# Hybrid decoder block on one Trainium2 core: the low part of every second MLP weight chunk made by an adding transfer instead of a subtraction

## Chip, cores and metric

The kernel runs on one core of one Trainium2 chip. The metric is device time in microseconds (us), the median of several executions; lower is better. Everything is float32 at the interface. The times of the kernel before are 1257.58, 1258.53 and 1259.71 us.

## The reference

One layer of a hybrid decoder trunk, for 256 tokens (and 16 learned meta tokens ahead of them) of width 2048:

```
u = RMSNorm(h)
[z_pool | v_conv | g_conv | gate_a | gate_b] = u @ W_in
A: causal multi-scale pooling, per-group map, scale, projection to 2048
B: GLU -> depthwise conv (31 taps) -> LayerNorm -> swish -> projection to 2048
m = sigmoid(gate_a) * A + sigmoid(gate_b) * B ;  h += RMSNorm(m @ W_o)
h += RMSNorm(W_down (relu(W_up RMSNorm(h)))^2)
```

The change touches only the last line, the MLP. `W_up` is 2048 x 8192 and `W_down` is 8192 x 2048, 64 MB each in float32.

## The kernel before

**Products in split precision.** Each float32 weight is split exactly into a high part (rounded to the short format `float32r`) and a low part (the rest), and so is each activation. A product is made of three: high by high, high by low, low by high. In `mm2` (L312 and L317) the high weights meet both parts of the activations in one matmul of 512 columns and the low weights meet the high activations in one of 256; in `block_t` (L651) there are three matmuls of 512 columns for every 128 rows of weights.

**Chunks.** All weights come in one fixed list, `stream`, of chunks of 1 MB: 128 partitions x 2048 floats. An MLP chunk holds 512 rows (4 tiles of 128) by 512 columns, so in HBM it is made of runs of 2 KB, and on chip each partition has one run of 8 KB. There are 217 chunks, numbered from 0; the MLP's are 89 to 216. The inner width of the MLP is taken in four pieces; each has 16 chunks of `W_up` (4 columns of 4 chunks, the "up" stages) and then 16 chunks of `W_down` (the "dn" stages).

**Life of a chunk.** `open_chunk` (L136) takes room in three pools of three buffers each, `raw`, `hi` and `lo`, which rotate by chunk number. SyncE's queue (SP) loads `raw` from HBM (L153). ScalarE (ACT) copies `raw` to `hi` with rounding (L156). VectorE (DVE) makes `lo = raw - hi` (L159). TensorE (PE) then reads `hi` and `lo`. `fetch` (L176) returns the next chunk for PE, and at the same time opens and splits the one two places further on. So the split of chunk c stands in the program ahead of PE's work on chunk c-2, and its `hi` and `lo` go into the room of chunk c-3: ACT waits for PE's end with chunk c-3, and PE then works through chunks c-2 and c-1 before it needs chunk c.

**Order.** Every engine issues in the order of the text (`manual_schedule`). SP issues only the chunk loads in this part of the kernel, one after the other: the load of chunk c+3 waits until the room of `raw` c is no longer read. ACT has, beside the casts to `hi`, in the up stages the copies of finished accumulators (`half_up`, L351) and the high parts of the MLP's activations (`f_act`, L358). GpSimd (POOL) is idle in the MLP; it issues a few transfers earlier in the kernel (L213, L679 to L683).

The last eight chunks (209 to 216) and the first eight of the MLP (89 to 96) are not touched by the change.

Of the kernel before, what the change touches and what calls it, by code (L numbers as in the profile page):

```python
# [11 lines left out]
ALU = mybir.AluOpType  # L12
# [3 lines left out]
CK = 4          # rows of 128 in one weight chunk  # L16
CW = 512        # columns of one weight chunk
# [5 lines left out]
def hybrid_block(ctx: ExitStack, tc: tile.TileContext, ins: dict, out: bass.AP):  # L23
# [6 lines left out]
    NT = T // P                     # token tiles  # L30
    KD = D // P                     # feature tiles of the model width
# [11 lines left out]
    KP = PW // P                    # feature tiles of the pooling branch  # L43
    KC = CC // P                    # feature tiles of the convolution branch
    FF = w_up.shape[1]
    PAD = TAPS - 1 - M              # zeros ahead of the first meta token
# [19 lines left out]
    # every engine issues in the order of this text  # L66
    ctx.enter_context(tc.manual_schedule())

# [1 line left out]
    pending = []  # L70
    late = []                       # what the Scalar engine does after the next chunk's split
    LATER = (0, None)               # what follows waits for the next call
    FETCH = (0, late)               # what follows waits for what is late
# [7 lines left out]
    def drain(us=None):  # L81
        """as much of it as fits in us, with what earlier calls left over"""
        credit["us"] += us or 0.0
        while pending and (us is None or credit["us"] >= pending[0][0]):
            cost, f = pending[0]
            if f is late and late:
                if us is not None:
                    break
                flush()
            pending.pop(0)  # L90
            if callable(f):
                f()
                if us is not None:
                    credit["us"] -= cost
            elif f is None and us is not None:
                break
        credit["us"] = min(credit["us"], pending[0][0]) if pending else 0.0

# [1 line left out]
    def columns(w, k0, nk, c0, shape=(CK, CW)):  # L100
        """chunks of rows k0.. (nk tiles), columns c0.., in their order"""
        ck, cw = shape
        return [(w[(k0 + kc) * P:(k0 + kc + ck) * P, c0:c0 + cw]
                 .rearrange("(k p) c -> p k c", p=P), shape) for kc in range(0, nk, ck)]
# [20 lines left out]
    # two chunks of w_up that are split early, into room that is free for a while  # L125
    spare = {len(stream) + 1: "s0", len(stream) + 2: "s1"}
    for i in range(NP):
        for h in range(NB):
            stream += columns(w_up, 0, KD, i * D + h * CW)
        for n in range(NB):  # L130
            stream += columns(w_down, i * KD, KD, n * CW)
    FIRST = KD // HALF[0]           # chunks of the first product, taken piece by piece
    opened = []                     # chunks under way
    at = {"n": 0}

    def open_chunk():  # L136
        n = at["n"]
        at["n"] += 1
        src, (rows, width) = stream[n]
        raw = raws.tile([P, CK * CW], F32, tag="raw", name=f"raw_{n}")  # L140
        if n in spare:
            both = big.tile([P, 2, CK * CW], F32R, tag=spare[n], name=f"parts_{n}")
            hi, lo = both[:, 0, :], both[:, 1, :]
        else:
            hi, lo = (parts.tile([P, CK * CW], F32R, tag=tag, name=f"{tag}_{n}")
                      for tag in ("hi", "lo"))
        raw, hi, lo = (t.rearrange("p (k c) -> p k c", k=rows) for t in (raw, hi, lo))
        pieces = rows if n < FIRST + 1 else 1
        k = rows // pieces
        loads = 4 if n < FIRST else 1  # L150
        for i in range(loads):
            sl = slice(i * rows // loads, (i + 1) * rows // loads)
            nc.sync.dma_start(raw[:, sl, :], src[:, sl, :])  # L153

        def high(sl):
            nc.scalar.copy(hi[:, sl, :], raw[:, sl, :])  # L156

        def low(sl):
            nc.vector.tensor_sub(lo[:, sl, :], raw[:, sl, :], f32(hi[:, sl, :]))  # L159

        def piece(i):
            def f():
                sl = slice(i * k, (i + 1) * k)
                high(sl)
                low(sl)
            return f
        todo = [piece(i) for i in range(pieces)]
        if n in spare:
            todo = [lambda: high(slice(0, rows)), lambda: low(slice(0, rows))]
        opened.append((hi, lo, todo))  # L170
# [5 lines left out]
    def fetch(ahead=2):  # L176
        """the next chunk, with the ones after it under way"""
        for c in range(ahead + 1):
            if c == len(opened) and at["n"] < len(stream):
                open_chunk()  # L180
            if c < len(opened):
                split_pieces(c)
        flush()
        return opened.pop(0)[:2]

# [7 lines left out]
    def warm_up(func):  # L193
        """loads the table of func"""
        nc.scalar.activation(warm, ones[:, 0:1], func)
# [21 lines left out]
    def rows_to_columns(rows, n, name):  # L217
        """vectors, P of their elements to a column"""
        pv = misc_tile(f"pv_{name}")
        nc.tensor.transpose(pv[:, :n], rows[:n, :], ident[:n, :n])  # L220
        nc.vector.tensor_copy(vecs[:, cols[name]:cols[name] + n], pv[:, :n])
# [20 lines left out]
    # the Tensor engine's clock rises with work: some of it until the data is there  # L242
# [25 lines left out]
    def rsqrt(r, q, var):  # L268
        """r: 1/sqrt(var), with q the table's root, after one of Newton's steps on it"""
# [32 lines left out]
    def mm3(acc, hi, lo, act, k, cs, first, last):  # L302
        """acc[:, :N] += w.T @ act, for the tokens in act or the last T of them, of the two
        parts of each"""
# [15 lines left out]
    def mm2(acc, hi, lo, act, k, cs, first, last):  # L320
        """acc[:, :T] + acc[:, T:] += w.T @ act, for the last T tokens, with the high part of
        the weights against both parts at once"""
# [9 lines left out]
    def project(act, nk, evac, name, mm=mm2, width=CW, shape=HALF, fill=0.0):  # L332
        """the next columns of act @ w; evac(j, acc) takes each P of them"""
# [14 lines left out]
    def halves(acc, name):  # L348
        """the two halves' sum, on chip"""
# [48 lines left out]
    # the first product: each tile of x as it comes, each chunk piece by piece  # L398
    def pieces_to(n):
        """the splits of the first n pieces"""  # L400
# [70 lines left out]
    def level(g):  # L471
        """trailing sums of 2 ** (g + 1) tokens, for the groups from g on"""
# [32 lines left out]
    ln = {}  # L505

    def sum_items(key, dst, src):
        """the sum over all channels, in every partition; dst is overwritten"""
# [19 lines left out]
    QW = 4                          # channel tiles to an instruction  # L528
# [134 lines left out]
    def project_t_but_two(act, nk, accs):  # L663
        """all but the last two chunks, which are returned"""
# [7 lines left out]
    def project_t_two(act, nk, accs, two, t):  # L672
        """the last two chunks, for one tile of tokens"""
# [12 lines left out]
    class Norm:  # L686
        """1/rms of the tokens of a tile, from the sums of squares of its blocks"""
# [10 lines left out]
        def steps(self, t, last=None):  # L698
            """1/rms, in steps: the root's table, and one of Newton's steps on it"""
# [51 lines left out]
    u2 = m                          # whose first tiles are read no more by then  # L751

    def u2_tiles(t0, n, k0, nk):
        """feature tiles k0.. of h1, for n tiles of tokens from t0 on: to features x tokens;
        returns what makes the parts of it"""
# [31 lines left out]
    # the first tokens are done two chunks earlier than the last ones in the last columns of w_o,  # L787
    # and go ahead of them in the first ones of w_up
# [46 lines left out]
    def up_high(kc, t):  # L835
        """the high parts of a chunk, for a tile of tokens"""
# [49 lines left out]
    # the norm's scale of a token goes through relu^2 as its square  # L886
# [37 lines left out]
    def finish_down(t, cuts):  # L924
        """the residual and the way out, in pieces of columns"""
# [13 lines left out]
    # the last columns: the first tokens are done three chunks earlier than the last ones, which  # L939
    # take their columns in two halves  # L940
# [65 lines left out]
```

## Time and profile before

| | |
|---|---|
| median of 3 runs | 1258.53 us |
| span of the profiled execution, first to last instruction | 1256.1 us |
| what lies around the span, against that median | 2.4 us |
| PE busy | 1242.3 us, 99% |
| DVE busy | 822.0 us, 65% |
| ACT busy | 544.7 us, 43% |
| chunk loads by SP (queue q1) | 230.70 MB, 57.7% of the 16 DMA engines' span |

The span is that of one execution under the profiler. No separate time of that execution is given outside the span, so the 2.4 us are the difference to the median of the unprofiled runs. A busy time counts an engine's instructions; its share says nothing about who waits for whom. That is read from the chain that ended last, from the timeline, and from the waits. The share of a DMA queue is the time that its packets took, divided by the time of all 16 engines: share times window is the time that the work would take with all 16 engines busy on it.

### The profile page before, as it was taken

Reading aid. Unit: us, or ns where it says so; the run is one execution under the profiler, and the core shown is the slowest. Engines: PE = TensorE matmul, PEld = TensorE weight load, DVE = VectorE, ACT = ScalarE, POOL = GpSimd, SP = SyncE. Lnnn points to the kernel's source line nnn. Section 1 sums busy time; section 2 is a strip of 40 time slices with the busy share of each in tenths; the row PEclk is TensorE's granted clock in tenths of the full one; section 3 lists DMA queues with packets and bytes.
Section 4 is the critical chain, followed back from the end, with each engine's and each line's share of the span. In section 5 each row is a group of like instructions: output and inputs, shape, how many; then the busy total and the mean of one; then the engine's idle time right before and its main releaser. Section 6 shows DMA issues by size and latency. Waiting matters only on the chain.

```text
span 1256.1 us, 18048 instructions
## 1 busy us (share of the span) xinstructions
PE 1242.3 (99%) x7682; PEld 1118.4 (89%) x7682; DVE 822.0 (65%) x1002; ACT 544.7 (43%) x595; POOL 6.1 (0%) x18
## 2 busy tenths in 40 slices
PE   8999999999999999999999999999999999999997
PEld 7999999999999988898888888888888888888886
DVE  5799986999887764585654456544475544556555
ACT  6633334443457444455433335433344433435432
POOL 1000000000000000000000000000000000000000
PEclk9999999999999999999999999999999999999999
DMA  8655556555656865646556656556656556666551
GB/s 244 208 184 179 168 175 195 175 195 177 193 168 212 290 203 194 207 137 199 179 191 200 194 177 198 175 194 200 189 180 200 177 194 200 178 191 198 180 192 68
DMA packets 155346, 237.39 MB, mean 189 GB/s; under 512 B 3986, under 2 KB 79058, under 8 KB 154737
## 3 DMA queue, kind: packets, MB, share of 16 engines
q1 hardware_dynamic: 153856, 230.70, 57.7%
q0 software_dynamic: 768, 4.35, 0.9%
q8 instruction: 60, 0.98, 0.3%
q10 hardware_dynamic: 640, 1.19, 0.3%
q14 instruction: 22, 0.17, 0.0%
HBM read 234.12 MB, written 2.10 MB: 188 GB/s over the span
## 4 chain that ended last, share of the span: by engine, by line
PE 98%; DMA 1%; DVE 0%; ACT 0%; DVEq 0%; ACTq 0%; issue 0%
PE acc_dn L651 26%; PE acc_up L312 19%; PE acc_gate L307 15%; PE acc_up L317 10%; PE acc_o L651 5%; PE acc_v L307 4%; PE acc_z L307 4%; PE acc_g L307 4%; PE acc_po L307 4%; PE acc_co L307 4%; PE acc_f_last L651 2%; PE acc_o_last L651 2%; PE xt L256 1%; DMA m_in<-in_meta_dram 1%; PE ht L759 0%; PE xt L254 0%
## 5 line engine op out<-in xcount | busy, mean ns | idle before, releaser
L159 DVE TENSOR_TENSOR lo<-raw,hi 128x2048 fp32r<-128x2048 f32 (+1 forms) x236 | 495.0, 2100 | 360.2 <-ACT hi L156 360.0
L156 ACT CAST hi<-raw 128x2048 fp32r<-128x2048 f32 (+1 forms) x236 | 413.9, 1757 | 583.6 <-PE acc_dn L651 191.1
L312 PE MATMUL acc_up<-m,hi 128*128 128x512 f32 (+1 forms) x1008 | 344.8, 395 | 0.0
L651 PE MATMUL acc_dn<-hi,f_act 128*128 128x512 f32 x960 | 295.9, 389 | 0.0
L317 PE MATMUL acc_up<-m,lo 128*128 128x256 f32 x992 | 265.8, 281 | 0.0
L312 PEld LDWEIGHTS acc_up<-m,hi 128*128 128x128 f32 x1008 | 183.3, 188 | 39.5
L651 PEld LDWEIGHTS acc_dn<-hi,f_act 128*128 128x128 f32 x960 | 180.2, 188 | 37.1
L317 PEld LDWEIGHTS acc_up<-m,lo 128*128 128x128 f32 x992 | 186.2, 189 | 6.3
L651 PE MATMUL acc_dn<-lo,f_act 128*128 128x512 f32 x480 | 186.7, 389 | 0.0
L307 PE MATMUL acc_gate<-u,hi 128*128 128x256 f32 x1024 | 182.9, 283 | 0.0
L307 PEld LDWEIGHTS acc_gate<-u,hi 128*128 128x128 f32 x1024 | 157.5, 189 | 0.1
L307 PE MATMUL acc_gate<-u,lo 128*128 128x256 f32 x512 | 144.7, 283 | 0.0
L375 DVE SCALAR_TENSOR_TENSOR c<-a,taps,c 128x256 f32<-128x256 f32 x240 | 115.2, 482 | 6.1
L651 PEld LDWEIGHTS acc_dn<-lo,f_act 128*128 128x128 f32 x480 | 90.1, 188 | 18.9
L307 PEld LDWEIGHTS acc_gate<-u,lo 128*128 128x128 f32 x512 | 97.0, 189 | 0.0
L651 PE MATMUL acc_o<-hi,m 128*128 128x512 f32 x192 | 59.3, 389 | 0.0
L307 PE MATMUL acc_v<-u,hi 128*128 128x272 f32 x256 | 50.8, 296 | 0.0
L307 PE MATMUL acc_g<-u,hi 128*128 128x272 f32 x256 | 48.4, 288 | 0.0
L307 PE MATMUL acc_z<-u,hi 128*128 128x272 f32 x256 | 48.3, 288 | 0.0
L307 PE MATMUL acc_po<-y,hi 128*128 128x256 f32 x256 | 45.5, 280 | 0.0
L307 PE MATMUL acc_co<-s_act,hi 128*128 128x256 f32 x256 | 45.3, 279 | 0.0
L651 PEld LDWEIGHTS acc_o<-hi,m 128*128 128x128 f32 x192 | 36.0, 188 | 7.5
(221 smaller groups left out, 1151.5 us busy)
## 6 DMA issues: line engine op xcount, KB each, us to landing
raw<-in_w_up_dram SPq DMA_DIRECT2D x64, 1024.0 KB, 5.4
raw<-in_w_down_dram SPq DMA_DIRECT2D x64, 1024.0 KB, 5.1
raw<-in_w_in_dram SPq DMA_DIRECT2D x54, 1024.0 KB, 5.1
raw<-in_w_o_dram SPq DMA_DIRECT2D x16, 1024.0 KB, 5.1
raw<-in_w_pool_out_dram SPq DMA_DIRECT2D x8, 1024.0 KB, 5.3
raw<-in_w_conv_out_dram SPq DMA_DIRECT2D x8, 1024.0 KB, 6.3
x_in<-in_x_dram SPq DMA_DIRECT2D x4, 512.0 KB, 8.8
raw<-in_w_in_dram SPq DMA_DIRECT2D x8, 256.0 KB, 7.7
```

Of the source, the lines that this page charges most:

```text
L156: nc.scalar.copy(hi[:, sl, :], raw[:, sl, :])
L159: nc.vector.tensor_sub(lo[:, sl, :], raw[:, sl, :], f32(hi[:, sl, :]))
L256: nc.tensor.transpose(pt[:, M + t * P:M + (t + 1) * P], x_in[:, t, sl], ident)
L307: nc.tensor.matmul(acc, w[:, k[0], cs], act[:, k[1], a, off:], start=first and n == 0, stop=last and n == 2)
L312: nc.tensor.matmul(acc.rearrange("p (a t) -> p a t", a=2)[:, :, ts], hi[:, k[0], cs], act[:, k[1], :, off + ts.start:off + ts.stop], start ...
L317: nc.tensor.matmul(acc[:, :T], lo[:, k[0], cs], act[:, k[1], 0, off:], start=False, stop=False)
L375: nc.vector.scalar_tensor_tensor(c, conv["a"][:, q, i:i + T], taps[:, q, i:i + 1], c, op0=ALU.mult, op1=ALU.add)
L651: nc.tensor.matmul(acc, act(kk)[:, a_, ts_], w_[:, k, :], start=kk == 0 and n == 0, stop=kk == nk - 1 and n == 2)
```

## The change

From chunk 97 on (`MLP0 = 89 + 8`) and up to chunk 208, every odd chunk gets its low part in another way. ACT, after the cast to `hi`, writes `-hi` into `lo` (float32r to float32r, scale -1). GpSimd then issues a transfer with `accum_op=add` that adds the raw weights to `lo`. For chunk numbers 97, 101, 105, ... (n % 4 == 1) the raw weights are read from the `raw` tile on chip; for 99, 103, ... (n % 4 == 3) they are read once more from HBM. These are 56 chunks, 28 of each sort. The even chunks keep the subtraction on DVE.

```
+    MLP0 = len(stream) + 8
...
         def low(sl):
+            if n >= MLP0 and n % 2 and n < len(stream) - 8:
+
+                nc.scalar.activation(lo, f32(hi), AF.Copy, scale=-1.0)
+                nc.gpsimd.dma_start(lo, raw if n % 4 == 1 else src, accum_op=ALU.add)
+                return
             nc.vector.tensor_sub(lo[:, sl, :], raw[:, sl, :], f32(hi[:, sl, :]))
```

The rest of the diff takes comments out. In the built program the DVE stream is shorter by 56 subtractions, ACT's is longer by 56 instructions, and POOL's by 56 transfers. PE's instructions are the same in the same order; 56 of them, the first that read such a `lo`, now wait for a transfer where they waited for DVE. On SP, the load of chunk c+3 waits for the adding transfer of chunk c where c is of the on-chip sort, and for ACT alone where c is of the HBM sort.

## The prediction

> **What bounds the kernel now.** I read the page's busy times first, then the chain that ended last, then a table by stretch of one dn group of four chunks and one up group.
>
> ```profile
> span 1256.1 us, 18048 instructions
> ...
> PE 1242.3 (99%) x7682; PEld 1118.4 (89%) x7682; DVE 822.0 (65%) x1002; ACT 544.7 (43%) x595; POOL 6.1 (0%) x18
> ...
> PE 98%; DMA 1%; DVE 0%; ACT 0%; DVEq 0%; ACTq 0%; issue 0%
> ```
>
> ```profile
> core 0: us, PE busy (x) PEld busy (x) DVE busy (x) ACT busy (x) POOL busy (x), PEclk, DMA share, GB/s
> 697.58:719.43 21.85, 21.85 (x105) 18.31 (x104) 10.46 (x6) 7.65 (x4) 0.00 (x0) 1.00 0.66 193
> 719.43:742.04 22.61, 22.61 (x130) 19.62 (x129) 13.61 (x16) 10.14 (x12) 0.00 (x0) 1.00 0.60 184
> ```
>
> TensorE is 98% of the chain and has no gap in either stretch, at full clock. VectorE and ScalarE have 0% of the chain. So work taken off VectorE buys nothing by itself. The question is only whether the new way to make `lo` is in time. ScalarE's timeline gives the pace of the chunks and VectorE's the present end of the split:
>
> ```profile
> 697.58 1.91 ACT L156 CAST hi<-raw 128x2048 fp32r<-128x2048 f32 x1 [3.52 <-PE acc_dn L651]
> 703.02 1.91 ACT L156 CAST hi<-raw 128x2048 fp32r<-128x2048 f32 x1 [3.53 <-PE acc_dn L651]
> 708.46 1.91 ACT L156 CAST hi<-raw 128x2048 fp32r<-128x2048 f32 x1 [3.53 <-PE acc_dn L651]
> ...
> 725.08 1.91 ACT L156 CAST hi<-raw 128x2048 fp32r<-128x2048 f32 x1 [3.73 <-PE acc_up L312]
> 730.73 1.91 ACT L156 CAST hi<-raw 128x2048 fp32r<-128x2048 f32 x1 [3.75 <-PE acc_up L312]
> ...
> 736.89 0.37 ACT L351 COPY half_up<-acc_up 128x256 f32<-128x256 f32 x1
> 737.15 1.91 ACT L156 CAST hi<-raw 128x2048 fp32r<-128x2048 f32 x1
> 738.96 0.72 ACT L358 CAST f_act<-sum_up 128x256 fp32r<-128x256 f32 x2
> 742.04 1.91 ACT L156 CAST hi<-raw 128x2048 fp32r<-128x2048 f32 x1 [2.37 <-PE acc_up L312]
> ```
>
> ```profile
> 704.97 2.29 DVE L159 TENSOR_TENSOR lo<-raw,hi 128x2048 fp32r<-128x2048 f32 x1 [3.15 <-ACT hi L156]
> ```
>
> A chunk takes TensorE 703.02 - 697.58 = 5.44 us in dn and 5.65 us in up (725.08 to 730.73); four take 21.8 and 22.6. The cast to `hi` of chunk c starts when TensorE leaves chunk c-3. TensorE needs chunk c two chunks later: **the cover is 10.9 us in dn, 11.3 in up**. Today cast and subtraction end 704.97 + 2.29 - 703.02 = 4.2 us after that start, so 6.6 us are spare. Once per up column the cast sits behind the column's evacuation: it starts at 737.15 where 730.73 + 5.65 = 736.4 was due, 0.8 us late. Columns begin at chunk numbers that are 1 modulo 4, and this cast is two places on: an odd chunk of the HBM sort.
>
> **The change part by part.**
>
> *Removed:* 56 subtractions on VectorE, 56 x 2.29 = 128 us. None stands on the chain: worth 0 to the end. *Added on ScalarE:* 56 negations.
>
> ```profile
> L156 ACT CAST hi<-raw 128x2048 fp32r<-128x2048 f32 x212 | 405.0, 1911 | 583.6 <-PE acc_dn L651 191.1 <-PE acc_up L312 146.6 <-issue 78.5
> ...
> L537 ACT ACTIVATE sq<-c 128x1024 f32<-128x1024 f32 x2 | 2.1, 1058 | 0.0
> ```
>
> No row has this operation in this size; the cast of equal size takes 1.91 us, an activation of half the size 1.06, so it lies between 1.9 and 2.1, and I take 1.95. That is 109 us more for ScalarE, some 650 of 1256: idle time covers it. Queued behind a negation are accumulator copies and `f_act` casts in up. The tightest place is the one quoted: the cast ends at 739.06, the negation at 741.0, the two `f_act` casts at 741.7, and the next cast is due at 742.04. It fits by 0.3 us; if it did not, the next chunk, an even one, has 6.6 us spare. I cost it at nothing there, but in the new path it counts in full: negation done 1.95 + 1.95 = 3.9 us after the cast's start, where the transfer is issued.
>
> *Added on GpSimd and the DMA engines:* 56 transfers of 1 MB. Nothing else waits on GpSimd's queue there. What do they cost? No accumulating transfer is in the trace. The rows for plain ones, first in a quiet part of the MLP, then where GpSimd issued three while chunk loads ran:
>
> ```profile
> q1 hardware_dynamic: 9167, 18.22, 58.5%
> ...
> raw<-in_w_down_dram SPq DMA_DIRECT2D x16, 1024.0 KB, 5.1
> ```
>
> ```profile
> q1 hardware_dynamic: 3472, 3.51, 52.8%
> q0 software_dynamic: 560, 4.19, 51.4%
> ...
> raw<-in_w_conv_out_dram SPq DMA_DIRECT2D x3, 1024.0 KB, 16.4
> h<-in_x_dram POOLq DMA_DIRECT2D x1, 2048.0 KB, 9.5
> g_mix<-in_g_post_mix_dram POOLq DMA_DIRECT2D x1, 1024.0 KB, 13.1
> g_mlp<-in_g_post_mlp_dram POOLq DMA_DIRECT2D x1, 1024.0 KB, 15.5
> ```
>
> ```profile
> 401.03 0.54 POOL L681 DMA_DIRECT2D g_mix<-in_g_post_mix_dram  x1
> ```
>
> The first two rows are of 600 to 695 us: 18.22 MB took 58.5% of 95 us, so a chunk (1.049 MB, runs of 2 KB) is 3.20 us of all 16 engines, and it lands 5.1 us after issue: 1.9 us of fixed delay. The others are of 400 to 420 us: GpSimd's queue moved 4.19 MB in 51.4% of 20 us, 2.57 us for a chunk's bytes in runs of 8 KB. An add must read `lo` as well as the raw weights before it writes, so **I charge two transfers' work**: 2 x 2.57 = 5.1 us for the on-chip sort (runs of 8 KB), 2 x 3.20 = 6.4 for the HBM sort. Bounds: one transfer's work (the second read hidden) and three (read, read, write in turn).
>
> The Trainium skill, "Collectives: The Full Stack", section "Part 3: Why 7× under link rate — side-by-side accounting", says that a DMA add gives two read descriptors to one queue where a copy gives one, and that reducing ran at half the rate of copying (32.35 against 62.28 GB/s). That was for rings between cores; nothing here shows it yet. By its factor of 1.93 the transfer below would land 0.2 us sooner and the sum would be 6 us less.
>
> Landing time of the HBM sort, the longer one: 1.9 fixed + 0.5 for GpSimd's issue (0.54 in the row) + 6.4 of work + what it shares. The load of chunk c+3 is freed by the cast alone (1.9 us after its start instead of 4.2), so it runs just ahead of the adding transfer: I charge one load of 3.2 us. Sum **L = 12.0 us**. By the rows the ends are 5.1 us (a load in quiet) and 16.4 (a load in the crowd); `h`, which reads 2 MB as an add does, took 9.5 and `g_mix`, queued behind it, 13.1. 12.0 lies between these two nearest rows.
>
> *The wait that this makes.* From cast to landing D = 3.9 + 12.0 = 15.9 us in dn, and 16.7 in up with the 0.8 of late cast, against covers of 10.9 and 11.3. The first matmuls on `lo` wait, with all of TensorE's queue behind them. But a wait ahead of chunk c also lengthens the cover of chunk c+2, whose cast starts when TensorE leaves c-1, before that wait. So the waits of the two sorts do not add. The loop that counts goes once round in four chunks: TensorE works two chunks (10.9 or 11.3), leaves the room, then D passes, and then chunk c+4 can start. Four chunks take at least 10.9 + 15.9 = 26.8 in dn (21.8 now, +5.0) and 11.3 + 16.7 = 28.0 in up (22.6 now, +5.4). Of the 28 groups from chunk 97 to 208 half are dn: 14 x 5.0 + 14 x 5.4 = **+146 us**.
>
> Engine time as a second bound: four loads and two adds are 4 x 3.20 + 5.1 + 6.4 = 24.3 us in four chunks. It is above today's 21.8 and 22.6, so the loads cannot hide the adds in full, and below 26.8, so the landing decides, with DMA 90% busy.
>
> *Moved on SP:* the load of chunk c+3 after an on-chip add waits for its landing, 3.9 + L against 4.2 before, and the load of c+4 is queued behind it. Chunk c+3 is even: load (5.1) and split (4.2) must be done within five chunks, 27.2 us after the cast of c, so an on-chip add may take 27.2 - 3.9 - 5.1 - 4.2 = 14.0 us. On-chip adds take 1.9 + 0.5 + 5.1 = 7.5 plus sharing: cost 0, and hidden under the HBM sort's longer wait.
>
> ```profile
> 417.62 1.91 ACT L156 CAST hi<-raw 128x2048 fp32r<-128x2048 f32 x1 [9.54 <-DMA raw<-in_w_conv_out_dram]
> ```
>
> ```profile
> 399.99 45.23 PE acc_co L307 x384
> ```
>
> These two rows, of the same crowd, show it: one cast came over 9 us late for want of its load, and TensorE's stretch in the chain has no break.
>
> The sum: 1256.1 + 146 = 1402 us of span, and with the 2.4 us around it (1258.53 - 1256.1) **1404 us**.
>
> **The rivals.**
>
> *In time after all (not slower).* If the second read is hidden and no load is in the way, L = 1.9 + 0.5 + 3.2 = 5.6 us. The point is L = 10.9 - 3.9 = 7.0 in dn, 6.6 in up. Below it TensorE waits nowhere: 1258.5 us. For it: a plain load lands in 5.1. Against it: `h` took 9.5. The Trainium skill, "DMA: Bandwidth & Descriptors", section "Anatomy of one DMA — SWDGE (gpsimd) path", has 2.0 us plus the bytes at 436 GB/s, an estimate of 4.4 us for 1 MB, and so speaks for this rival; for the 2 MB of `h` it gives 6.8 where the trace has 9.5 in the crowd.
>
> *One transfer's work, but behind a load.* L = 5.6 + 3.2 = 8.8: 14 x (1.8 + 2.2) = +56, 1315 us.
>
> *The DMA engines as the bound.* At three transfers' work four chunks need 12.8 + 3 x 5.8 = 30.1 us of all engines; L is 15.2, D + cover 30.0 and 31.2: 14 x (8.2 + 8.6) = +235, 1494 us. At four times, engine time alone (35.9 us) sets the pace: 14 x (14.1 + 13.3) = +384, 1642 us. For it: an add has three passes over SBUF or HBM, and loads held back by it come in bursts. Against it: `h` and its neighbours moved 7.7 MB in 20 us without a break on TensorE.
>
> **How the numbers follow.** Chances: two transfers' work, 1404 us, 0.51 (with sharing between none and 6.4 us, L = 8.8 to 15.2, so 1315 to 1494 by the sums above); one transfer's work behind a load, 0.12; in time, 0.05, of which 0.01 for a measurable gain, for which the profile has no source; three times, 0.20; four and more, 0.12. The range 1300 to 1600 leaves out the case in time and a little of its neighbour (some 0.08) and the dearest (some 0.11). Below 0.2% (2.5 us) a measurement cannot tell this kernel from no change. Faster 0.01, within 0.2% 0.04, slower 0.95.
>
> **What would show it.** In the changed kernel TensorE's busy share should fall to about 89%, with waits on the transfer into `lo`, mostly ahead of HBM-sort chunks and few ahead of on-chip ones. The issue table should give 12 us to landing for the HBM sort and 7.5 to 10 for the on-chip sort, GpSimd's queue about 28 x 11.5 = 320 us of all engines, the negation 1.9 to 2.1 us, and an unchanged 5.44 us per chunk where nothing waits. A landing under 7 us makes the forecast wrong downward; a queue with over twice the plain work makes it wrong upward; equal waits ahead of both sorts would refute the loop.

## The result, and the profile after

The changed kernel takes 1396.49 us (median of 4, 1390.74 to 1400.19) against 1258.87 for the kernel before: a ratio of 1.109, 95% interval 1.107 to 1.111. The forecast was 1404. The profiled execution has a span of 1388.9 us and a time of 1390.74.

The page of the changed kernel, at the places that were shown of before:

```profile
span 1388.9 us, 18258 instructions
...
PE 1284.7 (92%) x7682; PEld 1145.5 (82%) x7682; DVE 696.3 (50%) x946; ACT 651.0 (47%) x651; POOL 67.3 (5%) x74
...
q1 hardware_dynamic: 153856, 230.70, 50.3%
q0 software_dynamic: 19584, 63.07, 23.7%
...
PE 64%; DMA 20%; issue 9%; ACT 4%; DVE 2%; SPq 0%; POOLq 0%; DVEq 0%; ACTq 0%
...
lo<-raw POOLq DMA_DIRECT2D x28, 1024.0 KB, 7.0
...
lo<-in_w_up_dram POOLq DMA_DIRECT2D x14, 1024.0 KB, 9.4
lo<-in_w_down_dram POOLq DMA_DIRECT2D x14, 1024.0 KB, 8.6
```

TensorE was 98% of the chain and is 64%; the transfers into `lo` now make up nearly all of the 20% of DMA. TensorE's waits (engine and line, what it waited for, total, times, longest) say which ones:

```profile
PE acc_dn L657 <- DMA lo<-in_w_down_dram: 44.2, 14, 4.8
PE acc_up L323 <- DMA lo<-in_w_up_dram: 44.0, 14, 6.4
...
PE acc_up L323 <- DMA lo<-raw: 1.7, 1, 1.7
```

All 28 chunks of the HBM sort are waited for, and one of the on-chip sort: 89.9 us of wait. The span grew by 132.8. The other 42 us are in the matmuls: the same 7682 are busy for 1284.7 us, not 1242.3. The chain from 703 to 764 us (start, length, what) shows the loop of four chunks twice:

```profile
703.24 8.56 DMA lo<-in_w_down_dram
...
711.84 10.76 PE acc_dn L657 x46
...
722.63 4.36 issue
...
727.00 11.38 DMA lo<-in_w_down_dram
...
738.43 12.36 PE acc_dn L657 x46
...
750.82 4.36 issue
...
755.19 9.00 DMA lo<-in_w_up_dram
```

Transfer, two chunks of TensorE, 4.36 us from the freed room to the issue (cast, negation, two hand-overs), transfer again. Two things differ from one round to the next. The transfer lands after 8.6 us or after 11.4. And after the long wait the two chunks take 12.36 us, not 10.76. TensorE's timeline and a table by stretch at that place show how:

```profile
738.43 0.50 PE L657 MATMUL acc_dn<-lo,f_act 128*128 128x512 f32 x1 [4.51 <-DMA lo<-in_w_down_dram]
...
741.86 0.63 PE L657 MATMUL acc_dn<-lo,f_act 128*128 128x512 f32 x1
...
742.87 0.40 PE L657 MATMUL acc_dn<-lo,f_act 128*128 128x512 f32 x1
```

```profile
734.00:738.40 4.40, 0.00 (x0) 0.00 (x0) 0.00 (x0) 3.54 (x2) 0.54 (x1) 1.00 1.09 281
738.40:742.40 4.00, 3.97 (x11) 3.11 (x12) 0.00 (x0) 0.00 (x0) 0.35 (x1) 0.59 1.02 253
742.40:746.40 4.00, 4.00 (x19) 3.30 (x18) 0.00 (x0) 0.80 (x1) 0.00 (x0) 0.98 0.51 105
```

The third column from the end is the granted clock, as a share of TensorE's full clock (the last two are the DMA engines' share, which counts packets' time and can pass 1, and GB/s): 0.59 in the 4 us after a wait of 4.51 us, with 11 matmuls instead of 19, then 0.98 again.

### The profile page after: what moved, and what is told of

Its sections match the earlier page's. It is cut to its first block, busy times and chain, and to the rows that moved or that the text cites. A ratio compares the mean times of both kernels' runs of the same rounds, so it can differ in the third digit from the quotient of the medians.

```text
span 1388.9 us, 18258 instructions
## 1 busy us (share of the span) xinstructions
PE 1284.7 (92%) x7682; PEld 1145.5 (82%) x7682; DVE 696.3 (50%) x946; ACT 651.0 (47%) x651; POOL 67.3 (5%) x74
## 3 DMA queue, kind: packets, MB, share of 16 engines
q0 software_dynamic: 19584, 63.07, 23.7%
## 4 chain that ended last, share of the span: by engine, by line
PE 64%; DMA 20%; issue 9%; ACT 4%; DVE 2%; SPq 0%; POOLq 0%; DVEq 0%; ACTq 0%
PE acc_dn L657 13%; PE acc_gate L313 13%; DMA lo<-in_w_up_dram 10%; DMA lo<-in_w_down_dram 10%; PE acc_up L318 8%; PE acc_o L657 5%; PE acc_up L323 4%; PE acc_v L313 4%; PE acc_z L313 3%; PE acc_g L313 3%; PE acc_co L313 3%; PE acc_po L313 3%; ACT hi L157 3%; PE acc_f_last L657 2%; PE acc_o_last L657 2%
## 5 line engine op out<-in xcount | busy, mean ns | idle before, releaser
L165 DVE TENSOR_TENSOR lo<-raw,hi 128x2048 fp32r<-128x2048 f32 (+1 forms) x180 | 366.7, 2041 | 582.5 <-ACT hi L157 582.3
L318 PE MATMUL acc_up<-m,hi 128*128 128x512 f32 (+1 forms) x1008 | 364.8, 411 | 0.0
L323 PE MATMUL acc_up<-m,lo 128*128 128x256 f32 x992 | 277.6, 293 | 45.7 <-DMA lo<-in_w_up_dram 44.0
L657 PE MATMUL acc_dn<-hi,f_act 128*128 128x512 f32 x960 | 304.2, 398 | 0.0
L323 PEld LDWEIGHTS acc_up<-m,lo 128*128 128x128 f32 x992 | 196.9, 200 | 56.5 <-DMA lo<-in_w_up_dram 48.5
L657 PE MATMUL acc_dn<-lo,f_act 128*128 128x512 f32 x480 | 194.1, 404 | 44.2 <-DMA lo<-in_w_down_dram 44.2
L318 PEld LDWEIGHTS acc_up<-m,hi 128*128 128x128 f32 x1008 | 194.2, 199 | 41.8
L657 PEld LDWEIGHTS acc_dn<-hi,f_act 128*128 128x128 f32 x960 | 186.3, 194 | 39.2
L162 ACT ACTIVATE lo<-hi 128x2048 fp32r<-128x2048 f32 x56 | 107.2, 1915 | 1.8
L163 POOL DMA_DIRECT2D lo<-raw x28 | 24.8, 886 | 423.8 <-ACT lo L162 423.8
```

What stands on the lines that cost most here:

```text
L162: nc.scalar.activation(lo, f32(hi), AF.Copy, scale=-1.0)
L163: nc.gpsimd.dma_start(lo, raw if n % 4 == 1 else src, accum_op=ALU.add)
L318: nc.tensor.matmul(acc.rearrange("p (a t) -> p a t", a=2)[:, :, ts], hi[:, k[0], cs], act[:, k[1], :, off + ts.start:off + ts.stop], start ...
L323: nc.tensor.matmul(acc[:, :T], lo[:, k[0], cs], act[:, k[1], 0, off:], start=False, stop=False)
L657: nc.tensor.matmul(acc, act(kk)[:, a_, ts_], w_[:, k, :], start=kk == 0 and n == 0, stop=kk == nk - 1 and n == 2)
```

## The experiments

The theory after the result: **landing**. Four chunks take TensorE's two chunks plus the time from cast to landing of the transfer that lands latest, whatever the other sort does; slow matmuls after long waits come on top. The rivals: the **DMA engines are full** (their work sets the pace), and **waits add up** (each transfer brings its own). All runs in one table. "Waits" are TensorE's waits for transfers into `lo`, "more busy" is its busy time above 1242.3 us (in `fill` less the 76 us of filling); together they make up the difference of the spans to within 1 us in every run.

| kernel | median us | ratio (95%) | waits | more busy |
|---|---|---|---|---|
| as changed | 1396.5 | 1.107 to 1.111 | 89.9 | 42.4 |
| hbm_only | 1351.9 | 1.072 to 1.076 | 66.5 | 26.5 |
| all_hbm | 1347.3 | 1.068 to 1.073 | 67.7 | 21.0 |
| neg_first | 1365.4 | 1.083 to 1.086 | 75.0 | 32.8 |
| plain | 1288.2 | 1.023 to 1.026 | 21.3 | 8.9 |
| no_hold | 1346.7 | 1.066 to 1.075 | 67.8 | 24.8 |
| fill | 1385.4 | 1.098 to 1.104 | 36.3 | 19.4 |
| chip_only | 1297.2 | 1.030 to 1.033 | 27.6 | 11.1 |
| all_chip | 1392.6 | 1.105 to 1.113 | 90.3 | 35.5 |
| hbm_neg_first | 1324.2 | 1.051 to 1.055 | 46.3 | 19.6 |
| chip_no_hold | 1308.4 | 1.037 to 1.040 | 41.2 | 15.7 |
| neg_only | 1258.3 | 0.999 to 1.001 | 0 | 1.1 |
| all_hbm_neg_first | 1329.5 | 1.053 to 1.060 | 54.8 | 22.2 |

**The HBM sort alone (hbm_only).**

```
-            if n >= MLP0 and n % 2 and n < len(stream) - 8:
+            if n >= MLP0 and n % 4 == 3 and n < len(stream) - 8:
```

> Only the 28 chunks of the HBM sort get the adding transfer; the on-chip sort goes back to the subtraction. Landing theory (four chunks take the cover of two plus the time from cast to landing of the HBM sort): with no on-chip transfer in the way the landing is the shorter one seen, 8.6 us in dn and 9.0 in up, so 10.9 + 4.2 + 8.6 = 23.7 and 11.3 + 5.0 + 9.0 = 25.3 us for four chunks, 14 x (1.9 + 2.7) = +64: about 1323 us, with 28 waits of TensorE of 1.5 to 3 us. Rival, the DMA engines are full: four loads and one add are 4 x 3.2 + 6.4 = 19.2 us of engine time, under today's 21.8, so no wait and 1259 us. Rival, every add brings its own wait and waits add up: the 28 that remain keep 89 us of wait, 1350 us or more.

1352 us, above the 1323 of the landing theory and far from the 1259 of full engines. It is the time that the rival of adding waits named (1350 or more), but that rival had 89 us of wait and the run has 66.5. These are near the 64 that the landing theory expected; the rest, 26.5 us, is the slow matmuls, which the expectation left out. The next run parts the two. The chain of one round in a dn stage, link by link:

```profile
874.65 10.97 PE acc_dn L657 x47
...
885.64 1.92 ACT hi L157
...
887.59 1.93 ACT lo L162
889.52 0.28 issue
889.80 8.92 DMA lo<-in_w_down_dram
```

10.97 + 1.92 + 1.93 + 0.28 + 8.92 = 24.0 us against 21.8 before. The next round begins at 898.76, 24.1 after this one. The DMA engines' share of these 24.1 us is 0.76, so they were not what set the pace.

**All 56 from HBM (all_hbm).**

```
-                nc.gpsimd.dma_start(lo, raw if n % 4 == 1 else src, accum_op=ALU.add)
+                nc.gpsimd.dma_start(lo, src, accum_op=ALU.add)
```

> All 56 adding transfers read the raw weights from HBM. Landing theory with its loop of four chunks: the second set of waits lies beside the first, and only the landing counts: at 9 to 11.4 us the time is 1390 to 1440. Engines full: 12.8 + 2 x 6.4 = 25.6 us of work in four chunks where the changed kernel has 24.3: +1.3 x 28 = +36, about 1430. Waits add up: 56 waits of the size that 28 have now, 1259 + 2 x 137 = about 1530 us.

1347 us: below what every theory gave, the 1390 to 1440 of the landing theory too, and no more than with 28 transfers. Twice as many transfers wait no longer in total (45 waits, 67.7 us, against 28 and 66.5), as the loop has it and against adding waits. And the queue did more work than in the changed kernel in less time:

```profile
q0 software_dynamic: 30336, 63.07, 27.0%
```

27.0% of 1345 us are 363 us of all engines against 23.7% of 1389, 329 us. So full engines did not set the pace of the changed kernel. What is missing here is the on-chip sort.

Whether the engines set the pace of all_hbm itself stays open. Their share from 600 to 1250 us (last column but one) is 0.89 in the changed kernel and 1.00 in all_hbm:

```profile
600.00:1250.00 650.00, 573.61 (x2715) 478.93 (x2716) 181.77 (x219) 306.91 (x245) 53.30 (x49) 0.94 0.89 236
```

```profile
600.00:1250.00 650.00, 589.97 (x2897) 488.42 (x2896) 197.94 (x246) 328.93 (x269) 66.45 (x52) 0.98 1.00 249
```

At the prediction's prices four chunks are 4 x 3.20 + 2 x 6.4 = 25.6 us of all engines, 3.4 more than the 22.2 that they took before (the mean of dn and up). That is 95 us in 28 rounds, 1354 us, close to the 1347 measured.

**The room that the on-chip sort holds (no_hold).** The load of chunk c+3 waits until an on-chip add has read `raw`. This run adds another tile of the same shape instead, so the add stays and the hold goes.

```
-                nc.gpsimd.dma_start(lo, raw if n % 4 == 1 else src, accum_op=ALU.add)
+                other = g_mlp.rearrange("p (k c) -> p k c", k=rows)
+                nc.gpsimd.dma_start(lo, other if n % 4 == 1 else src, accum_op=ALU.add)
```

> The 28 on-chip transfers add another tile on chip of the same shape (the gain vector of the last norm, which stays in SBUF) in place of raw: same bytes, same paths, but the room of raw is free after the cast. The low parts of those chunks are left wrong. Theory, the held room: the load of chunk c+3 waits for the on-chip add, the loads then come in a bunch and every second HBM-sort transfer runs against them (11.4 us to landing in place of 8.6). Without the hold all HBM-sort transfers land in 8.5 to 9.5 us and the time is that of the kernel with HBM alone as the source, 1335 to 1355 us. Rival, the on-chip add itself is what costs: nothing changes, 1390 to 1400 us. Rival, the DMA engines are full: nothing changes either.

1347 us, as the held room has it. The issue table:

```profile
lo<-g_mlp POOLq DMA_DIRECT2D x28, 1024.0 KB, 9.8
lo<-in_w_up_dram POOLq DMA_DIRECT2D x14, 1024.0 KB, 9.3
lo<-in_w_down_dram POOLq DMA_DIRECT2D x14, 1024.0 KB, 8.5
```

The transfers between 690 and 960 us that come from HBM land after 8.3 to 9.7 us one like the other, where six of the changed kernel's ten from 703 to 940 us take 8.4 to 9.4 and four take 10.9 to 11.9. The DMA packets from issue to landing show what lies beside them. These are the chunk loads (q1) beside the transfers of 8.56 us (703.24 to 711.80) and of 11.38 us (727.00 to 738.38):

```profile
q1 hardware_dynamic: 581, 1.16, 35.2%
```

```profile
q1 hardware_dynamic: 1168, 2.33, 56.3%
```

1.16 MB is about one chunk, 2.33 MB more than two. Over the ten it is 1.1 to 1.3 MB beside the six and 2.0 to 2.5 beside the four. In no_hold it is 0.9 to 1.3 MB from 690 to 960 us.

The on-chip transfers land later without the hold (9.8, before 7.0), since the next load is no longer kept away from them, and TensorE waits for 18 of them, 16.6 us in all; its waits for the HBM sort fall from 88.2 to 51.2 us. So **50 of the 138 us come from the hold**: it adds no wait of a cast for a load in the changed kernel, but held loads go out in a bunch against the next HBM-sort transfer. SP's waits in the changed kernel show its size:

```profile
SPq L154 <- DMA lo<-raw: 344.9, 28, 14.4
```

**The on-chip sort alone, with and without the hold (chip_only, chip_no_hold), and for all 56 (all_chip).** The first two have `n % 4 == 1` in the condition, the second adds `other` as above; the third adds `raw` for every odd chunk.

> Only the 28 chunks of the on-chip sort get the adding transfer; the HBM sort goes back to the subtraction. Landing theory: 7.0 us after issue, 4.2 + 7.0 = 11.2 after the cast, against a cover of 10.9 in dn and 11.3 in up: waits of 0.3 us or none, 1259 to 1266 us. If holding back the loads costs by itself, or if each add brings its share of the loss, half of it stays: about 1320 us.

> All 56 adding transfers read raw on chip. Landing theory with 7.0 to 7.8 us: 4.2 + 7.4 = 11.6 in dn against 10.9, 12.4 against 11.3 in up with the late cast: 14 x (0.7 + 1.1) = +25, about 1284 us. With every odd chunk holding its room the loads bunch more, and the landing goes to 8 or 9 us: 1300 to 1330. Engines full: 12.8 + 2 x 5.1 = 23.0 us in four chunks against 21.8 and 22.6: +22, about 1281 us.

> Only the on-chip sort, adding the other tile on chip in place of raw, so that the room of raw is free after the cast (the low parts of those chunks are left wrong). Theory, the held room makes the 39 us that the on-chip sort costs alone: 7 to 8 us to landing, 1259 to 1268 us. Rival, the add's traffic in SBUF makes them: 1290 to 1300 us.

All three missed: 1297, 1393 and 1308 us. In a quiet dn stretch of chip_only the landing theory holds:

```profile
856.80 6.92 DMA lo<-raw
...
863.76 15.14 PE acc_dn L657 x66
...
878.90 6.94 DMA lo<-raw
```

22.1 us a round, 0.3 over the 21.8 of before. But in the up stages the transfer lands after 9.1 us, and a load is in the chain there, for which ScalarE waits:

```profile
ACT hi L157 <- DMA raw<-in_w_up_dram: 29.8, 7, 5.4
```

```profile
769.49 8.53 DMA raw<-in_w_up_dram
...
784.23 9.15 DMA lo<-raw
```

So held loads come late enough to hold up casts, and with the cast everything behind it on ScalarE. The later landing has another source. The hold keeps the loads away from the transfer in both stages: from 784.23 to 793.38 us q1 moves nothing, and beside the transfer's own packets stands one of another queue, `instruction`, which the window of 856.80 to 863.72 does not have:

```profile
q8 instruction: 1, 0.02, 0.6%
```

18 of the 28 transfers have such a packet before their landing and take 7.2 to 9.2 us; the ten without take 6.9. That this packet is the cause is not tried. Without the hold the loads do run beside the transfer: the issue table of chip_no_hold has

```profile
lo<-g_mlp POOLq DMA_DIRECT2D x28, 1024.0 KB, 8.8
```

and the time is worse by 11 us, not better: the hold is harmful where an HBM-sort transfer follows, and in sum not for the on-chip sort by itself. With all 56 on chip ScalarE waits for 32 loads in the MLP, and landings run from 7.2 to 12.9 us between 690 and 960.

The two sorts alone cost 38 and 93 us, nearly the 138 of both together. That looks like adding waits, but without the hold they cost 50 and 93 alone and 88 together. So the sum is chance: the loop takes the longer of the two, and the hold puts 50 on top.

**The add's price (plain).**

```
-                nc.gpsimd.dma_start(lo, raw if n % 4 == 1 else src, accum_op=ALU.add)
+                nc.gpsimd.dma_start(lo, raw if n % 4 == 1 else src)
```

> The 56 transfers copy the raw weights into lo and do not add; the add is left out, so lo holds the raw weights. It tells the price of the add. Two transfers' work for an add: GpSimd's queue falls from 318 us of all engines to about 160 for the 56 transfers, the HBM sort lands in 5.5 to 8.8 us in place of 8.6 to 11.4, and the time is 1259 to 1300 us. One transfer's work: queue time, landing and the 1396 us stay.

1288 us, in the range expected for two transfers' work, with

```profile
q0 software_dynamic: 19584, 63.07, 14.5%
...
lo<-raw POOLq DMA_DIRECT2D x28, 1024.0 KB, 4.2
...
lo<-in_w_up_dram POOLq DMA_DIRECT2D x14, 1024.0 KB, 7.3
lo<-in_w_down_dram POOLq DMA_DIRECT2D x14, 1024.0 KB, 6.9
```

14.5% of 1286 us less the 11 us of the other transfers is 175 us for 56, 3.13 us each; with the add it is 318 us, 5.68 each: 1.81 times. The Trainium skill, "Collectives: The Full Stack", section "Part 3: Why 7× under link rate — side-by-side accounting", has reducing at 1/1.93 of copying, for a ring between cores; these runs inside one core come near it.

**Sooner by one instruction (neg_first, hbm_neg_first, all_hbm_neg_first).** The first, for the mixed sorts; the other two have `src` for all and, in hbm_neg_first, `n % 4 == 3`.

```
         def high(sl):
+            if n >= MLP0 and n % 2 and n < len(stream) - 8:
+                nc.scalar.activation(lo, raw, AF.Copy, scale=-1.0)
+                nc.gpsimd.dma_start(lo, raw if n % 4 == 1 else src, accum_op=ALU.add)
             nc.scalar.copy(hi[:, sl, :], raw[:, sl, :])
...
-                nc.scalar.activation(lo, f32(hi), AF.Copy, scale=-1.0)
-                nc.gpsimd.dma_start(lo, raw if n % 4 == 1 else src, accum_op=ALU.add)
```

> The negation is made from the raw weights, ahead of the cast (lo = -raw rounded, the same values), so that the transfer is issued 1.9 us sooner; the same transfers with the same bytes. Landing theory: cast to landing is 1.9 us shorter, 28 x 1.9 = 53 us less, and the slow matmuls after long waits go too (up to 40 us less): 1300 to 1345 us. Engines full: the work is the same, 1390 to 1400 us.

> Only the HBM sort, with the negation made from the raw weights ahead of the cast, so that the transfer is issued 1.9 us sooner. Landing theory: 2.2 + 8.5 = 10.7 against 10.9 in dn, 3.0 + 9.1 = 12.1 against 11.3 in up: 14 x 0.8 = +11, about 1270 us, and up to 1290 if the landing is later by the 1.4 us that it was with both sorts. Rival, the engines' work is what counts: the same work as with the HBM sort alone, 1352 us.

> All 56 transfers read HBM, and the negation is made from raw ahead of the cast. It is the kernel with the change that the runs so far make the best. Landing theory: 1347 - 28 x 1.9 = 1294 us if the landing stays at 8.4 to 10 us; 1310 to 1330 if it comes 1 us later, as it did with both sorts. Engines full (25.6 us of work in four chunks, so +3.4 x 28 = 95 at the least): 1347 us and no gain.

31, 28 and 18 us less than without, where the issue alone is worth 53; the first two miss the landing theory's ranges and the third is at the upper end of the later-landing one. The transfers land later. In hbm_neg_first:

```profile
raw<-in_w_up_dram SPq DMA_DIRECT2D x64, 1024.0 KB, 5.8
raw<-in_w_down_dram SPq DMA_DIRECT2D x64, 1024.0 KB, 6.0
...
lo<-in_w_up_dram POOLq DMA_DIRECT2D x14, 1024.0 KB, 10.7
lo<-in_w_down_dram POOLq DMA_DIRECT2D x14, 1024.0 KB, 9.8
```

against 9.2 and 8.5 in hbm_only, and loads at 5.8 and 6.0 against 5.4 and 5.2. The round agrees with the loop: 10.9 + 2.2 + 9.8 = 22.9 us, and issues stand 22.6 to 23.1 us apart between 831 and 900. So some two thirds of the 1.9 us are given back. The order of issues changes: in hbm_only the load of chunk c+3, which the cast frees, goes out some 2 us ahead of the transfer and lands after 5.8 us (the one at 863.8 us); in hbm_neg_first it goes out some 1.6 us behind it and lands after 9.8 (at 832.5). That these two hinder each other is argued from the times, not tried. "Engines full" predicted no gain at all, which is not so in the first two. In all_hbm_neg_first, with a DMA share of 0.99, it stays possible: q1 spent 47.5% of 600 to 1250 us on 110.42 MB, against 49.8% on 107.79 MB in all_hbm, so four loads took 0.9 us less of the engines, 24 us in 28 rounds, where the gain is 18.

**Filling the wait (fill).**

```
+            for _ in range(12):
+                nc.tensor.matmul(spin, hi[:, 0, :P], hi[:, 1, :], start=True, stop=True)
```

> The changed kernel with twelve needless matmuls of 512 columns (12 x 0.227 = 2.7 us) on TensorE ahead of each of the 28 HBM-sort chunks, where it waits now. Theory, the slow matmuls after a wait are the granted clock, which falls when TensorE stands still for 3 us or more: they go (42 us of busy time), against some 0.5 us a time where the wait was shorter than the filling: 1350 to 1375 us with 336 more matmuls. Rival, they are slowed by the transfers that run beside them: they stay, and the filling adds to the short waits: 1396 to 1415 us.

1385 us, 11 less than as changed, 10 short of the range expected. The mean granted clock rises from 0.966 to 0.987 and the slow matmuls go from 42 to 19 us, with the same transfers beside them: it is the clock, and it follows the standing still. But the 76 us of filling take the place of only 54 us of wait, so that in the two profiled executions (1387.9 and 1388.9 us) the gain is all given back; these are the slowest of fill and the fastest of the changed kernel, and in the medians 11 us are left.

**The negation alone (neg_only).** The transfer and the `return` go; VectorE subtracts as before.

```
-                nc.gpsimd.dma_start(lo, raw if n % 4 == 1 else src, accum_op=ALU.add)
-                return
```

> The 56 negations on ScalarE stay, the transfers go, and VectorE makes lo of these chunks by the subtraction as before, after the negation. Negation and subtraction end 6.2 us after the cast's start, against 10.9: no wait, 1258 to 1260 us if the negation costs nothing; more if it holds up the copies behind it on ScalarE.

1258.3 us, ratio 0.999 to 1.001: 107 us more of ScalarE cost nothing.

## Why the prediction was right

- **The bound and the loop: right.** TensorE waits for the HBM sort (28 of 29 waits), a round is two chunks plus cast to landing, and the waits of two sorts do not add (all_hbm against hbm_only, no_hold against hbm_only and chip_no_hold). The DMA engines, forecast as 90% busy, have 0.89 from 600 to 1250 us.
- **The add as two transfers' work: right.** 5.1 and 6.4 us were charged. chip_only has 12.1% of 1295 us less 11, by 28: 5.2. hbm_only has 13.8% of 1349 less 11, by 28: 6.2.
- **Landing, 12.0 us: mis-sized.** The 28 HBM-sort transfers took 8.3 to 14.2 us, 9.8 in the mean; eight took 10.5 or more. The step that failed is the sharing: a whole load was charged in full, 3.2 us on top of delay, issue and work (8.8 us). The transfer at 703 us had one chunk of loads beside it and landed after 8.56 us, which is what the sum gives without any load; the one at 727 had two and landed after 11.38. Some 2.2 us too much in 28 rounds: 63 us.
- **From freed room to issue, 3.9 us: short.** It is 4.36, for the hand-overs between engines: 28 x 0.46 = 13 us too little.
- **The cost that was missing.** Nothing in the sum stood for slower matmuls after a wait: 42 us. Together -63 + 13 + 42 = -8, and the span came out 13 us under the forecast; the other 5 us are not accounted for. That the total was this much nearer than its terms is luck.
- **The hold on SP, costed at 0: wrong.** The sum of the prediction asked whether chunk c+3 would be in time. It did not ask what its late load would run against. no_hold shows 50 us. They came in through the landing that had been charged too high, and so did not show in the total.
- **The negation at nothing: right** (neg_only; 1.92 us each, as charged).
- **Rivals.** "In time after all" and "one transfer's work" fell with the price of the add; even hbm_neg_first, with the shortest path, misses the cover. "Engines as the bound" stood on three transfers' work for an add, and plain shows 1.81. No version tried beats the kernel before, and none was likely to, as the work taken off VectorE was not waited for.
- **Signs.** GpSimd's queue did 318 us of work for the 56 transfers (some 320 forecast). TensorE's share is 92% (89), and the on-chip sort lands after 7.0 us in the median (7.5 to 10).

## What to carry to other kernels

Before moving work off an engine that is not on the chain, work out the time from freed room to finished data on the new path, and compare it with the cover, that is, the work that the bottleneck has in between. A transfer's landing is no constant: ask which other transfers run in the same microseconds, and which of them the new one holds back, because held loads come out together. When the bottleneck is TensorE, charge a wait at more than its length (here 42 us of slow matmuls on 90 us of wait).

## What was not expected of the hardware

The granted clock falls after some surprisingly short waits. In hbm_only, after a wait of 2.27 us the next 5 us had a clock of 0.66, and after one of 1.76 us 1.00 (stretch, length, then busy times, and the clock third from the end):

```profile
849.20:854.20 5.00, 4.99 (x15) 3.93 (x16) 1.77 (x1) 0.00 (x0) 0.00 (x0) 0.66 0.82 281
874.60:879.60 5.00, 4.95 (x22) 4.10 (x23) 2.29 (x1) 0.00 (x0) 0.00 (x0) 1.00 0.66 221
```

The Trainium skill, "TensorE: Matmul & The Clock Gate", section "HAM oscillation — how this bites in real kernels", warns of gaps of over about 3.4 us. These traces show the fall after shorter ones. In hbm_only 12 of TensorE's 28 waits for `lo` were followed by 5 us at 0.66 or less, the shortest being this one of 2.27 us; after one of 2.56 us the clock stayed at 1.00. In all_hbm a wait of 1.78 us was followed by 0.66 too:

```profile
787.96:792.96 5.00, 5.00 (x20) 4.34 (x21) 1.43 (x4) 3.08 (x4) 1.28 (x1) 0.66 0.89 290
```

So the length of a wait alone does not tell whether the clock falls, and the 3 us that the expectation of fill supposed are no bound.
